# A decoder layer on Trainium2: a pool of its own for the output tile, another order at the start of the last stage, and other PSUM banks for the last blocks

## The chip, the cores and the metric

One core of a Trainium2 chip runs the whole program. The metric is the device time of one execution in microseconds (us); the kernel before took 1507.32 us, the median of three runs (1504.97 to 1509.54). Work is spread over TensorE (PE; its weight loads PEld), VectorE (DVE), ScalarE (ACT), GpSimd (POOL) and SyncE (SP), which only starts DMAs here. A line such as L1580 is line 1580 of the kernel before; the changed kernel counts its lines anew, so that L1277 of before is L1287 of after.

## The reference

One layer of a hybrid decoder in float32, for a prompt of 4096 tokens and a sample batch of 8 x 8 tokens, width 1024:

```python
h = _rmsnorm(x, g_pre)
z = h @ w_in
cb, cc, ch, cg, q, k, v, ag, mq, mg = _split_cols(z)
...
out_b = jax.nn.silu(ag) * o_b      # banded attention, window 128, 8 heads, 2 key-value heads, a sink each
out_c = jax.nn.silu(mg) * o_c      # cross attention into 256 memory tokens, 4 heads
y = jnp.concatenate([out_a, out_b, out_c], axis=-1) @ w_out
return x + _rmsnorm(y, g_post)
```

out_a is a gated short convolution. Keys, values and the last convolution rows are outputs too.

## The kernel before, in words

**Numbers.** Each float32 operand of a large product is split into a rounded part hi and the rest lo, and a product is three matmuls (hi with hi, lo with hi, hi with lo). A tile named mh or hi is the rounded part, ml or lo the rest.

**Stages one to three: the input projection.** The projection is cut into 2 x 2 blocks and done with seven products instead of eight (A for the weights, B for the activations, S and T for sums of them). The tokens go through in eight blocks, the weight columns in three groups. Products gather in PSUM banks as tiles c; DVE and ACT evict them into tiles z (L380, L382), which DMAs store to a tensor qd in DRAM. The first two blocks of tokens are done by a plain scheme (`plain_block`, a table of work by block and step). For block 2 the RMS factor of each row is to stand along the free axis: POOL forms the factors r (L293), `rows_diag` multiplies five columns of them into an identity matrix (L305; the tile is the memory of mix_s, 104 x 104 each), and PE multiplies ones with that (`rows_product`, L314, tile rows_y). In step (1, 4) of the table `rows_diag` stands behind the lo parts of a block of activations (L593) and some sums of weights (L606 to L618).

**The last stage: attention and output projection.** It has 33 blocks of 128 tokens (the 31st to run, b = 30, is followed by the sample block b = 32, then b = 31). A turn of the loop runs `Block.run` of block i: two accumulators y{b}_0 and y{b}_1 of 512 columns, each eight steps k of three matmuls with the weights wo. Between the steps the loop puts other work, by a table of events keyed (p, k): half of the output and step. At (0, 0), `values_and_scores(i)` does the scores of group i+3 (tiles ws in banks 0 to 3, xs in banks 4 and 5) and the values of group i+1 (tile pv, a pair of banks of its own). From group 3 on the softmax weights s are transposed by DVE in 32 x 32 squares and brought into place by 16 DMAs each (w<-s, L1268, on SP); POOL multiplies the cross weights by their reciprocal sums (L1232) and masks w and its copy wd (L1277, `masks`) before PE uses them (`values`). Group 2 is transposed by PE instead (`transposes`, tiles wt in banks 0 and 1, xt in banks 2 and 4, copied out into a tile w by L1286 and L1299).

A block's end: DVE multiplies y by gpost into yn (L1587), ACT sums the squares of y (L1588), and only after that is y's bank free; POOL forms the scale yst (L1601) and adds the scaled yn to the residual xr (L1608); SP stores it. From block 1 on y{b}_1 is the second bank of the pv pair. The tile yn comes from the pool yp, which is opened on memory that earlier tiles leave.

**What sets the order.** DMAs wait in SP's, ACT's or POOL's queue, each in order. A scheduler orders each engine's instructions by their readiness, but those that are issued through `InOrder`, or given to `tc.keep_in_program_order`, stay as written. Before, V (DVE) and TE (PE) were in order from block 1 to block 30 of the loop, S (ACT) only at single calls. In block 0, thus, readiness decided.

**The sample tokens** are worked into blocks 26 to 30 as generators (`sample_mem` twice, `sample_window`), one stage at each event of the table `sample`. They use bank 1 (svnt), 2 (smo) and 3 (sms, smt, smot), and loads svm and place<-in_cmv (L1419) on POOL's queue.

**Loads.** For chunk c (256 tokens) kst and q are loaded by POOL's queue from qd (L1087, L1093) in `chunk_load`, an event of every second block; vh (L1121) by SP.

## Time and profile before

| | us |
|---|---|
| median of three runs | 1507.32 |
| the profiled execution | 1511.43 |
| its span | 1509.7 |
| PE busy | 1475.2 (98%) |
| DVE busy | 1204.0 (80%) |
| ACT busy | 762.1 (50%) |
| POOL busy | 415.5 (28%) |

The mean granted clock of PE is 0.993 of full speed. Instructions are shown with start and length in us, engine, line, operation, output and inputs, shapes and count; behind it in brackets the idle time before it and whose work ended that. Matmuls overlap, so that a row's length can reach over the start of the next.

### The profile page before, as it was taken

Reading aid. Unit: us, or ns where it says so; the run is one execution under the profiler, and the core shown is the slowest. Engines: PE = TensorE matmul, PEld = TensorE weight load, DVE = VectorE, ACT = ScalarE, POOL = GpSimd, SP = SyncE. Lnnn points to the kernel's source line nnn. Section 1 sums busy time; section 2 is a strip of 40 time slices with the busy share of each in tenths; the row PEclk is TensorE's granted clock in tenths of the full one; section 3 lists DMA queues with packets and bytes.
Section 4 is the critical chain, followed back from the end, with each engine's and each line's share of the span. In section 5 each row is a group of like instructions: output and inputs, shape, how many; then the busy total and the mean of one; then the engine's idle time right before and its main releaser. Section 6 shows DMA issues by size and latency. Waiting matters only on the chain.

```text
span 1509.7 us, 30823 instructions
## 1 busy us (share of the span) xinstructions
PE 1475.2 (98%) x11479; PEld 1347.0 (89%) x11479; DVE 1204.0 (80%) x1888; ACT 762.1 (50%) x1878; POOL 415.5 (28%) x557
## 2 busy tenths in 40 slices
PE   9999999999999999999999999899999999999988
PEld 9999999999999999999999999777777777877656
DVE  5769888898998877798677668788888888898733
ACT  5776666466422222244544436556556566556531
POOL 0223322211400000000000111255665565665521
PEclk9999999999999999999999999899999999999999
DMA  9979999887764333388976797978999998998742
GB/s 258 172 244 226 288 277 271 236 284 246 190 221 168 134 121 129 109 276 266 307 226 206 228 281 257 303 203 207 241 238 236 226 223 218 247 229 206 237 127 94
DMA packets 212363, 334.18 MB, mean 221 GB/s; under 512 B 54517, under 2 KB 126197, under 8 KB 212181
## 3 DMA queue, kind: packets, MB, share of 16 engines
q1 hardware_dynamic: 170117, 259.30, 57.2%
q0 software_dynamic: 41376, 71.86, 19.9%
q8 instruction: 91, 1.49, 0.4%
q10 hardware_dynamic: 720, 1.05, 0.2%
q14 instruction: 59, 0.48, 0.1%
HBM read 192.54 MB, written 110.15 MB: 200 GB/s over the span
## 4 chain that ended last, share of the span: by engine, by line
PE 81%; DVE 6%; issue 5%; DMA 4%; ACT 2%; POOL 1%; SPq 0%; DVEq 0%; POOLq 0%; ACTq 0%
PE c L373 50%; PE y L65 19%; PE pv L65 5%; PE ws L65 3%; PE xs L65 1%; DMA wr_0A<-in_w_in 1%; DMA qd<-z 1%; PE mem_acc L789 1%; PE y L1580 1%; DMA vd<-v 1%; DVE s L65 1%; DVE z L380 0%; DVE wo L196 0%; DMA place<-in_xt 0%; ACT s L1207 0%
## 5 line engine op out<-in xcount | busy, mean ns | idle before, releaser
L65 PE MATMUL y<-wo,mh 128*128 128x512 f32 x960 | 307.8, 395 | 0.0
L380 DVE TENSOR_TENSOR z<-c,z 128x520 f32<-128x520 f32 (+1 forms) x308 | 194.3, 644 | 92.9 <-PE c L373 92.1
L65 PEld LDWEIGHTS y<-wo,mh 128*128 128x128 f32 x960 | 180.5, 188 | 51.0 <-issue 4.4
L65 PE MATMUL y<-wo,ml 128*128 128x512 f32 x480 | 187.3, 390 | 0.0
L1207 ACT ACTIVATE s<-s,wnm 128x128 f32<-128x128 f32 x256 | 99.0, 388 | 42.1 <-DVE wnm L65 39.0
L1232 POOL TENSOR_SCALAR s<-s,xrd 128x256 f32<-128x256 f32 x128 | 61.2, 491 | 166.5 <-DVE xrd L65 99.9
L65 PEld LDWEIGHTS y<-wo,ml 128*128 128x128 f32 x480 | 90.3, 188 | 17.6
L1190 ACT COPY s<-ws 128x256 f32<-128x256 f32 x128 | 41.2, 378 | 95.2 <-PE ws L65 74.2
L1608 POOL TENSOR_TENSOR xr<-yn,xr 128x1024 f32<-128x1024 f32 x31 | 74.3, 2397 | 20.8 <-ACT yn L1607 20.6
L748 POOL MEMSET negs<- 128x1 f32 x1 | 0.1, 98 | 264.3 <-PE c L373 264.3
L65 DVE STREAM_TRANSPOSE s<-s 128x1024 f32<-128x1024 f32 x56 | 68.4, 1238 | 2.5 <-POOL s L1232 2.5
L1277 POOL TENSOR_SCALAR_AFFINE_SELECT wd<-w 128x512 f32<-128x512 f32 (+1 forms) x58 | 54.2, 935 | 39.4 <-DMA w<-s 15.2
L1588 ACT ACTIVATE y<-y 128x512 f32<-128x512 f32 (+1 forms) x66 | 38.6, 585 | 52.1 <-DVE yn L65 43.3
L1224 ACT ACTIVATE s<-xs,xnm 128x256 f32<-128x256 f32 x128 | 58.1, 460 | 7.9 <-DVE xnm L1222 7.0
L65 DVE TENSOR_TENSOR yn<-y,gpost 128x512 f32<-128x512 f32 x60 | 41.0, 684 | 24.9 <-PE y L65 23.2
L65 PEld LDWEIGHTS ws<-kst,q 64*128 64x128 f32 x672 | 43.1, 190 | 17.4 <-issue 9.5
L65 PE MATMUL ws<-kst,q 64*128 64x256 f32 x672 | 49.5, 293 | 7.0 <-ACT w L1286 6.5
L65 DVE COPY_PREDICATED s<-wmask,ws 128x256 f32<-128x256 uint8 x112 | 43.5, 441 | 11.8 <-ACT s L1190 7.5
L382 ACT COPY z<-c 128x520 f32<-128x520 f32 (+1 forms) x44 | 24.4, 554 | 54.1 <-PE c L373 51.4
L1607 ACT ACTIVATE yn<-yn,yst 128x1024 f32<-128x1024 f32 x31 | 35.6, 1149 | 27.8 <-POOL yst L1601 27.8
L286 ACT ACTIVATE nat<-nat 104x1024 f32<-104x1024 f32 x40 | 42.2, 1054 | 12.9 <-DMA nat<-in_x_p 12.9
L1207 ACT ACTIVATION_READ_ACCUMULATOR s<-s,wnm 128x1 f32 x256 | 47.9, 187 | 0.0
(995 smaller groups left out, 5015.5 us busy)
## 6 DMA issues: line engine op xcount, KB each, us to landing
w<-s SPq DMA_DIRECT2D x464, 64.0 KB
q<-qd POOLq DMA_DIRECT2D x32, 768.0 KB, 8.2
xr<-in_x_p SPq DMA_DIRECT2D x32, 512.0 KB
nat<-in_x_p SPq DMA_DIRECT2D x39, 416.0 KB
o_yp<-xr SPq DMA_DIRECT2D x31, 512.0 KB
md<-th POOLq DMA_DIRECT2D x48, 260.0 KB, 6.6
qd<-zh SPq DMA_DIRECT2D x48, 260.0 KB
qd<-z SPq DMA_DIRECT2D x48, 260.0 KB
```

Of the source, the lines that this page charges most:

```text
L65: return (lambda *args, **kw: tc.keep_in_program_order(fn(*args, **kw))) if InOrder.on else fn
L286: S.activation(t[:RG], t[:RG], AF.Square, accum_out=r[:RG, i : i + 1])
L373: TE.matmul(bank[:, :HW], l, r, start=first and i == 0, stop=last and i == 3 * KH - 1)
L380: add = lambda dst, other: V.tensor_tensor(dst, c, other, op=ALU.add)
L1190: S.copy(to, squares(s3[:, :, P : 2 * P]))
L1207: S.activation(sm[:, h], sm[:, h], AF.Exp, bias=nm[:, h : h + 1], scale=SCALE, accum_out=den[:, h : h + 1])
L1224: S.activation(p[:, i], s[:, i].rearrange("p (a k j) -> p a k j", a=2, k=4), AF.Exp, bias=nm[:, i : i + 1], scale=SCALE, accum_out=den[:, ...
L1232: G.tensor_scalar(p[:, i], p[:, i], rd[:, i : i + 1], 0.5, op0=ALU.mult, op1=ALU.mult)
L1277: G.affine_select(out, src, pattern=[[32 * sign, 2], [0, 8], [sign, 32]], compare_op=op, fill=0.0, base=base * sign, channel_multiplier=-s ...
L1588: square = lambda acc=acc, p=p, c0=c0, c1=c1, end=end: S.activation((psum(2, "sq") if end else acc)[:m, : c1 - c0], acc[:m], AF.Square, sc ...
L1607: tc.keep_in_program_order(S.mul(yn, yn, st[:, 3:4]))
L1608: G.tensor_tensor(self.xr, yn, self.xr, op=ALU.add)
```

## The change

It has six parts.

1. In step (1, 4) of the plain scheme `rows_diag` goes ahead of the lo parts.
2. The tile yn comes from a new pool yq, opened before the others of its side; the pools vp and yp move with it.
3. Block 0 runs in program order on DVE and PE (`InOrder.on`), and on ACT as well (`InOrder.first`, block 0 alone). Its events are written anew: the transposes of group 2 come first, in banks 2 to 5 (the second cross transpose at (0, 3)), the values and scores at (0, 4); `weights(3)` is taken out of `values_and_scores` and put at (1, 0); the second square transposes of group 3 move to block 1; the split of block 1 is done in two halves.
4. The loads kst and q of chunks from 4 on stay in program order on POOL.
5. In the sample work the svm and cmv loads go to ACT's queue, the copy of smask comes behind the cwv load, svnt uses bank 5, and two stages of the first generator come later: (27, 1, 6) and (28, 0, 5) become (28, 0, 2) and (28, 1, 2). The mix of chunk 15 is loaded at (28, 0, 3) instead of (28, 0, 1).
6. y28_1, y29_1 and y30_1 use bank 5, and the sample block's accumulators banks 3 and 5.

```diff
-            return (lambda *args, **kw: tc.keep_in_program_order(fn(*args, **kw))) if InOrder.on else fn
-    V, TE = InOrder(nc.vector), InOrder(nc.tensor)
+            on = InOrder.first if self.engine is nc.scalar else InOrder.on
+            return (lambda *args, **kw: tc.keep_in_program_order(fn(*args, **kw))) if on else fn
+    V, TE, S = InOrder(nc.vector), InOrder(nc.tensor), InOrder(nc.scalar)
...
-            (1, 4): lambda: [*row, *parts(1, "B22"), *gains(2, "B11"), *sums(2, 1), lambda: rows_diag(), lambda: rows_bank(2),
+            (1, 4): lambda: [*row, lambda: rows_diag(), *parts(1, "B22"), *gains(2, "B11"), *sums(2, 1), lambda: rows_bank(2),
                              *fills(2, "S2"), *row],
...
+        yq = ctx.enter_context(tc.tile_pool(name="yq", bufs=1, side="right"))
         vp = ctx.enter_context(tc.tile_pool(name="vp", bufs=4, side="right"))
         yp = ctx.enter_context(tc.tile_pool(name="yp", bufs=2, side="right"))
...
+        def in_turn(self, ins):
+            if self.c > 3:
+                tc.keep_in_program_order(ins)
...
-                G.dma_start(self.q[:, :, part, :], qd[part, 1:7, :, self.ts].rearrange("j p n -> p j n"))
+                self.in_turn(G.dma_start(self.q[:, :, part, :], qd[part, 1:7, :, self.ts].rearrange("j p n -> p j n")))
...
-        def transposes(self):
+        def transposes(self, n):
+            if n:
+                self.cross_transposes(1, psum(5, f"xt{self.b}_1"))
+                return
...
-                self.band_transposes(u, psum(u, f"wt{self.b}_{u}"))
-            for u in range(2):
-                self.cross_transposes(u, psum(2 + 2 * u, f"xt{self.b}_{u}"))
+                self.band_transposes(u, psum(2 + u, f"wt{self.b}_{u}"))
+            self.cross_transposes(0, psum(4, f"xt{self.b}_0"))
...
-            (S.copy if u else V.tensor_copy)(self.xpt[u], t)
+            (S.copy if u or self.b == 2 else V.tensor_copy)(self.xpt[u], t)
...
-            groups[g].band_weights()
-            for u in range(2):
-                groups[g].cross_weights(u)
+            if i:
+                weights(g)
+            else:
+                blocks[1].split(1)
...
-            G.dma_start(vm[:, j], a["cmv"][j][:, bs])
+            tc.keep_in_program_order(S.dma_start(vm[:, j], a["cmv"][j][:, bs]))
...
-        G.tensor_copy(msk, raw)
...
+        tc.keep_in_program_order(G.tensor_copy(msk, raw))
         svn = vp.tile([P, P], F32, tag="v", name="svn")[:64]
-        transpose_to(svn, [(zs[:, 5, :], 64)], 1, "svnt")
+        transpose_to(svn, [(zs[:, 5, :], 64)], 5, "svnt")
...
-            yn = yp.tile([P, D], F32, tag="yn", name=f"yn{b}", bufs=1)
+            yn = yq.tile([P, D], F32, tag="yn", name=f"yn{b}")
...
+                elif b == 32:
+                    acc = psum(3 + 2 * p, f"y{b}_{p}")
+                elif p == 1 and 28 <= b < 31:
+                    acc = psum(5, f"y{b}_1")
...
-        at(0, 0 if i else 3, values_and_scores, i)
+        if i == 0:
+            at(0, 0, lambda: groups[2].transposes(0))
+            at(0, 3, lambda: groups[2].transposes(1))
+            at(1, 0, weights, 3)
+        if i == 1:
+            at(0, 0, turn, 1, 3)
+        at(0, 0 if i else 4, values_and_scores, i)
...
-        InOrder.on = 0 < i < 31
+        InOrder.on, InOrder.first = i < 31, i == 0
```

**DVE, the plain scheme.** At about 84 us DVE stands at the end of the sums of weights (wa). Before, it goes on like this, where mix_s are the products of `rows_diag` and lo0_1B22 the lo parts:

```order
L614 TENSOR_TENSOR wa2A21_1179<-wa2A11_1185,wa2A21_1179 128x512
L593 TENSOR_SCALAR lo0_1B22_1207<-x0_1B22_813,gpre_61,hi0_1B22_1206 128x260 x4
L606 TENSOR_TENSOR wa2A12_1232<-w0_2A12_451 128x512
L618 TENSOR_TENSOR wa2A12_1232<-wa2A12_1232,wa2A22_1181 128x512
L305 TENSOR_SCALAR mix_s_75<-ident_63,r2_915 104x104 x5
L196 TENSOR_TENSOR w0_2S2_1266<-wa2A22_1181,w0_2S2_1266 128x512
```

In the changed kernel the same place reads:

```order
L615 TENSOR_TENSOR wa2A21_1179<-wa2A11_1185,wa2A21_1179 128x512
L306 TENSOR_SCALAR mix_s_75<-ident_63,r2_915 104x104 x5
L594 TENSOR_SCALAR lo0_1B22_1224<-x0_1B22_813,gpre_61,hi0_1B22_1223 128x260 x4
L607 TENSOR_TENSOR wa2A12_1250<-w0_2A12_451 128x512
L619 TENSOR_TENSOR wa2A12_1250<-wa2A12_1250,wa2A22_1181 128x512
L197 TENSOR_TENSOR w0_2S2_1266<-wa2A22_1181,w0_2S2_1266 128x512
```

mix_s has moved ahead of the four lo parts and two sums of weights.

**PE, the start of the last stage.** Before, PE went from the last product c2_7_2_6 straight to y0_0, and the transposes of group 2 (wt2, xt2) stood inside the second half of block 0:

```order
L1580 MATMUL y0_1_12254<-wo1_1_11952,ml0_11992 128x512
L1580 MATMUL y0_1_12254<-wo1_1_11952,mh0_11991 128x512
L1285 MATMUL wt2_0_12263<-ident_63,s2_11356 128x128 x4
L1285 MATMUL wt2_1_12272<-ident_63,s2_11356 128x128 x4
L1298 MATMUL xt2_0_12280<-ident_63,s2_11356 128x128 x4
L1298 MATMUL xt2_1_12286<-ident_63,s2_11356 128x128 x4
L1580 MATMUL y0_1_12254<-wo2_1_11955,mh0_11991 128x512
```

In the changed kernel they follow the last product, where L66 is the line of the wrapper that keeps the order:

```order
L374 MATMUL c2_7_2_6_12020<-hi2_7T4_11919,w2_2A22_8593 128x260
L66 MATMUL wt2_0_12132<-ident_63,s2_11356 128x128 x4
L66 MATMUL wt2_1_12141<-ident_63,s2_11356 128x128 x4
L66 MATMUL xt2_0_12149<-ident_63,s2_11356 128x128 x4
L66 MATMUL y0_0_12129<-wo0_0_11764,mh0_11991 128x512
L66 MATMUL y0_0_12129<-wo0_0_11764,ml0_11992 128x512
```

Three of the four transposes have moved ahead of all of y0_0; xt2_1 comes behind its third step.

**POOL, a pair of blocks in the middle.** Before, the loads of chunk 5 (kst5, q5) stand around the addition to xr3, ahead of the weights of s7 (xrd are reciprocal sums); AFFINE_SELECT are the masks:

```order
L1601 TENSOR_TENSOR yst3_12749<-yst3_12749,mhalf_70 128x1
L1087 DMA kst5_13083<-qd_150 128x2x384
L1093 DMA q5_13085<-qd_150 128x6x256
L1608 TENSOR_TENSOR xr3_12452<-yn3_12748,xr3_12452 128x1024
L1093 DMA q5_13085<-qd_150 128x6x256
L1232 TENSOR_SCALAR s7_12959<-s7_12959,xrd7_0_13055 128x2x4x32 x2
L1232 TENSOR_SCALAR s7_12959<-s7_12959,xrd7_1_13063 128x2x4x32 x2
L1277 AFFINE_SELECT wd6_13117<-w6_12916 128x512
```

In the changed kernel:

```order
L1624 TENSOR_TENSOR yst3_12752<-yst3_12752,mhalf_70 128x1
L1631 TENSOR_TENSOR xr3_12455<-yn3_12751,xr3_12455 128x1024
L1240 TENSOR_SCALAR s7_12962<-s7_12962,xrd7_0_13058 128x2x4x32 x2
L1240 TENSOR_SCALAR s7_12962<-s7_12962,xrd7_1_13066 128x2x4x32 x2
L1089 DMA kst5_13086<-qd_150 128x2x384
L1099 DMA q5_13088<-qd_150 128x6x256 x2
L1287 AFFINE_SELECT wd6_13120<-w6_12919 128x512
```

The three loads have moved behind the weights of s7 and stand right ahead of the masks of group 6.

More of the change, by code (lines that the diff above doesn't have):

```diff
@@ L53, in hybrid_layer @@
     nc = tc.nc
-    S, G, DMA = nc.scalar, nc.gpsimd, nc.sync
+    G, DMA = nc.gpsimd, nc.sync
     class InOrder:
-        on = False
+        on = first = False
         def __init__(self, engine):
@@ L1012, in open_attention @@
     def open_attention():
-        nonlocal ps, mixp, wp, wl, vp, bp, bq, yp
+        nonlocal ps, mixp, wp, wl, vp, bp, bq, yp, yq
         own.close()
@@ L1165, in scores @@
             self.crosses(cross)
+            if self.b == 3:
+                blocks[1].split(0)
             self.band_softmax()
@@ L1368, in values_and_scores, with weights @@
                 groups[g].cross_softmax(cross[u], u)
-            groups[g].band_weights()
-            for u in range(2):
-                groups[g].cross_weights(u)
+            if i:
+                weights(g)
+            else:
+                blocks[1].split(1)
+    def weights(g):
+        groups[g].band_weights()
+        for u in range(2):
+            groups[g].cross_weights(u)
     tails = []
@@ L1555, in split @@
             src = chunks[b // 2].mix[:, :, (b % 2) * P : (b % 2) * P + P]
-            hi, lo = parts(f"mh{b}"), parts(f"ml{b}")
-            copy = S.copy(hi, src)
-            if 0 < b < 31:
-                tc.keep_in_program_order(copy)
-            V.tensor_tensor(lo, src, f(hi), op=ALU.subtract)
-            self.hl = [hi, lo]
+            if part != 1:
+                self.hl = hi, lo = parts(f"mh{b}"), parts(f"ml{b}")
+                copy = S.copy(hi, src)
+                if 1 < b < 31:
+                    tc.keep_in_program_order(copy)
+            if part != 0:
+                hi, lo = self.hl
+                V.tensor_tensor(lo, src, f(hi), op=ALU.subtract)
         def run(self, last, events):
             b, m = self.b, self.m
-            yn = yp.tile([P, D], F32, tag="yn", name=f"yn{b}", bufs=1)
+            yn = yq.tile([P, D], F32, tag="yn", name=f"yn{b}")
             dst = a["o_ys"] if b == 32 else a["o_yp"][b * P : (b + 1) * P, :]
@@ L1649, in events_of @@
             if i == 28:
-                at(0, 1, lambda: chunks[15].load_mix())
+                at(0, 3, lambda: chunks[15].load_mix())
         elif (i + 3) // 2 < NCH - 1:
             at(0, 3, lambda: chunks[(i + 3) // 2].load_mix())
-        if i == 0:
-            at(1, 2, lambda: groups[2].transposes())
         at(1, 1, turn, 2, i + 2)
@@ L1658, in events_of @@
         at(1, 2, turn, 0, i + 3)
-        at(1, 2, turn, 1, i + 3)
-        if i + 1 < len(blocks) and blocks[i + 1].b != 32:
-            at(1, 3 if i else 4, blocks[i + 1].split)
+        if i:
+            at(1, 2, turn, 1, i + 3)
+            if i + 1 < len(blocks) and blocks[i + 1].b != 32:
+                at(1, 3, blocks[i + 1].split)
         for (n, p, k), stage in sample.items():
```

8 lines of the change are left out of this document (4 added, 4 removed).

## The prediction

> **What bounds the kernel now.** I read the list of waits of TensorE first, then a table of stretches of the span, then the timelines around the three stretches that stand out. A row of waits gives who waited on which line, for whom, and total us, times, longest.
>
> ```profile
> PE pv L65 <- ACT y L1588: 6.7, 4, 4.2
> PE ws L65 <- ACT w L1286: 6.5, 1, 6.5
> PE rows_y L314 <- DVE mix_s L305: 2.2, 1, 2.2
> PE pv L65 <- POOL w L1277: 1.8, 2, 1.2
> PE y L1580 <- ACT y L1588: 1.6, 1, 1.6
> PE sws L65 <- ACT svn L1398: 1.4, 1, 1.4
> ```
>
> These six groups are 20.2 us. The page's first part has PE busy 1475.2 of 1509.7 us, so all its idle time is 34.5 us, and nothing can be won but that and what a lowered clock costs behind it. In the table, the columns behind a stretch are its length, the busy us of PE, PEld, DVE, ACT and POOL, the granted clock, the DMA share and GB/s.
>
> ```profile
> 86.00:94.00 8.00, 6.00 (x34) 5.83 (x35) 4.87 (x12) 5.38 (x11) 0.00 (x0) 0.79 0.87 236
> 970.00:982.00 12.00, 5.38 (x40) 4.66 (x42) 9.19 (x19) 8.24 (x29) 6.27 (x11) 0.62 1.28 363
> 1006.00:1400.00 394.00, 393.01 (x2844) 310.52 (x2844) 348.22 (x613) 235.56 (x856) 232.15 (x294) 1.00 0.91 227
> 1440.00:1452.00 12.00, 7.77 (x43) 5.04 (x42) 4.99 (x7) 3.32 (x6) 4.11 (x4) 0.72 0.59 153
> 1464.00:1500.00 36.00, 32.88 (x178) 25.70 (x177) 12.89 (x28) 9.25 (x18) 6.43 (x5) 1.00 0.26 88
> ```
>
> From 1006 to 1400 us PE idles 1.0 us of 394: the middle of the last stage is bound by TensorE's own work, which the change leaves as it is, so a gain must come from elsewhere. Three short stretches ran at a granted clock of 0.79, 0.62 and 0.72, each behind a PE gap of over 2 us. I call them A (86 us), B (970 us) and C (the end, from 1400 us); the change touches all three, and the middle as well.
>
> **A: the five mix_s products ahead of the lo parts.**
>
> ```profile
> 81.15 1.51 POOL L293 TENSOR_TENSOR r<-r,mhalf 104x5 f32<-104x5 f32 x1
> 84.29 1.68 DVE L593 SCALAR_TENSOR_TENSOR lo_1B<-x_1B,gpre,hi_1B 128x260 fp32r<-128x260 f32 x4
> 87.22 1.00 DVE L305 TENSOR_SCALAR mix_s<-ident,r 104x104 f32<-104x104 f32 x5
> 88.00 1.38 PE L314 MATMUL rows_y<-mix_s,ones 104*128 104x260 f32 x4 [2.25 <-DVE mix_s L305]
> ```
>
> The factors are there at 82.66 (81.15 + 1.51), and DVE reaches this place at 84.3. With mix_s first it runs from 84.3 to 85.3; PE wants it at 88.00 - 2.25 = 85.75. The gap of 2.25 us goes, and with it the clock drop, 8.00 x (1 - 0.79) = 1.7 us: 3.9 us in all. The four lo parts come 1.0 us later; their readers on PE stand behind rows_y and the w_1A and w_2A products with the part before, and these hide it; without that cover it costs 1.0 us. No instruction is added. I take **3.5 us**, between 2.9 and 3.9.
>
> **B: the start of the last stage.**
>
> ```profile
> 953.85 0.28 PE L373 MATMUL c<-hi_7T,w_2A 128*128 128x260 f32 x1
> 956.53 0.42 DVE L380 TENSOR_TENSOR z<-c,z 128x260 f32<-128x260 f32 x1
> 969.28 0.39 PE L1580 MATMUL y<-wo,mh 128*128 128x512 f32 x1
> 970.85 0.69 DVE L1587 TENSOR_TENSOR yn<-y,gpost 128x512 f32<-128x512 f32 x1 [6.48 <-DMA qd<-z]
> 975.57 1.05 ACT L1286 COPY w<-wt 128x512 f32<-128x512 f32 x2
> 976.19 2.13 PE L65 MATMUL ws<-kst,q 64*128 64x256 f32 x13 [6.53 <-ACT w L1286]
> 985.01 0.50 PE L65 MATMUL y<-wo,mh 128*128 128x512 f32 x1
> ```
>
> The chain reads backwards: ws4 waits 6.53 us for bank 0, which the copy of wt2 frees; ACT comes to that copy only at 975.57, since its exponentials waited for DVE; and DVE sat 6.48 us at yn0, whose memory lay over z tiles still being stored. With a pool of its own yn0 waits no longer. The copy of wt2 comes ahead of the scores on ACT, and the transposes use banks 2 to 5, so ws4 needs no release from them.
>
> What is late next is at the front. The first transposes now stand ahead of y0_0, in a bank that the last projection tile leaves by DVE's z eviction, done at 956.95, whereas PE ends its products at 954.13. Before, y0_0 filled these 2.8 us; now PE idles there. Its work from there to the old gap is the same and took 969.67 - 954.13 = 15.5 us, so PE is through at 957.0 + 15.5 = 972.5.
>
> The next group, ws4 to y1, took 985.01 - 976.19 = 8.8 us at a lowered clock and with a 0.43 us wait. What it takes at full clock is shown one block on:
>
> ```profile
> 996.11 1.70 PE L65 MATMUL ws<-kst,q 64*128 64x256 f32 x24
> 998.46 1.09 PE L65 MATMUL pv<-w,mv 128*64 128x128 f32 x16
> 999.38 1.03 PE L65 MATMUL pv<-w,vh 128*64 128x256 f32 x8
> 1000.94 0.50 PE L65 MATMUL y<-wo,mh 128*128 128x512 f32 x1
> 994.49 2.26 POOL L1277 TENSOR_SCALAR_AFFINE_SELECT w<-w 128x512 f32<-128x512 f32 x2
> ```
>
> It is 1000.94 - 996.11 = 4.8 us. y1 would start at 972.5 + 4.8 = 977.3. One wait is left in between: bank 3 holds y0_1 until DVE's product (0.69) and ACT's Square (0.58, row at 1443.85 below) have followed its last matmul, about 1.3 us: 978.6, or 985.0 - 978.6 = 6.4 us earlier. Two things may eat of this. The masks of w3 ended at 996.75 with their reader at 999.38, a cover of 2.6 us; a reader that comes 6.4 us sooner waits up to 3.8 us, unless the loads ahead of the masks come sooner too. They follow DVE work that stood behind yn0's wait, so they move by most of it: I take 0.7. And a gap of 2.8 us can lower the clock, as 2.25 us did at A for 1.7 us, while the two gaps of 1.6 us between 1464 and 1500 (clock 1.00) did not: two in five, 0.7 us. B gives **5.0 us**; its ends are 1 (3.8 and 1.7 lost) and 8 (most of the new gap gone).
>
> The Trainium skill ("TensorE: Matmul & The Clock Gate", section "Part 1: The HAM clock gate (the "warmup" mystery)") puts the drop behind at least one idle window of about 3.4 us. By it A's gap of 2.25 us would not have lowered the clock, and the row with 0.79 says that it did; for the new gap at 954 the rule gives no drop and B 5.7, by the row at A up to 1.7 us more is lost and B is 4.0. I go by the row.
>
> **The middle: POOL's loads.** For the twelve chunks from 4 on, three load issues move on POOL to between the weights of s and the masks. A row of a line gives min/median/max ns.
>
> ```profile
> L1093 POOL DMA_DIRECT2D q<-qd x32: 818/858/928, 718.4 to 1357.2; - x32
> 1137.56 1.84 POOL L1232 TENSOR_SCALAR s<-s,xrd 128x256 f32<-128x256 f32 x4 [4.64 <-DVE xrd L65]
> 1140.56 2.61 POOL L1277 TENSOR_SCALAR_AFFINE_SELECT wd<-w 128x512 f32<-128x512 f32 x2 [1.16 <-DMA o_yp<-xr]
> 1143.23 1.39 POOL L1277 TENSOR_SCALAR_AFFINE_SELECT w<-w 128x512 f32<-128x512 f32 x2
> 1144.17 1.17 PE L65 MATMUL pv<-w,vh 128*64 128x256 f32 x8
> ```
>
> The issues of a chunk (kst once, q twice) take about 3 x 0.86 = 2.6 us. Weights end at 1139.40, so masks could start at 1142.0, not 1140.56. The first w mask ended at 1143.93 and PE read at 1144.17: the cover is 0.24 us. Full shift: 1.44 - 0.24 = 1.2 us a block, 14 us for twelve. But the wd pair took 2.61 us here and 1.51 us at 992.91 to 994.42 in another block, so in part it was waiting in any case; 1.5 us from 1142.0 ends at 1143.5, 0.3 us later than before, about 0.1 over the cover. That is the nearer row. On the other side the loads no longer share the DMA engines with the w loads that precede these masks, which may end an idle us there. I take **-1.5 us**, ends -14 and +1. The loads themselves are read two blocks later or more, and come late for nobody.
>
> **C: the end.**
>
> ```profile
> 1439.69 2.36 DVE L65 STREAM_TRANSPOSE s<-s 128x1024 f32<-128x1024 f32 x2
> 1441.97 1.18 DVE L65 TENSOR_TENSOR ml<-place,mh 128x1024 fp32r<-128x1024 f32 x1
> 1443.08 0.68 DVE L65 TENSOR_TENSOR yn<-y,gpost 128x512 f32<-128x512 f32 x1
> 1443.85 0.58 ACT L1588 ACTIVATE y<-y 128x512 f32<-128x512 f32 x1 [2.36 <-DVE yn L65]
> 1444.59 1.98 PE L65 MATMUL pv<-w,mv 128*64 128x128 f32 x16 [4.23 <-ACT y L1588]
> 1449.26 0.79 PE L65 MATMUL y<-wo,mh 128*128 128x512 f32 x1
> 1457.40 1.40 POOL L1277 TENSOR_SCALAR_AFFINE_SELECT w<-w 128x512 f32<-128x512 f32 x2
> 1466.28 1.09 PE L65 MATMUL pv<-w,mv 128*64 128x128 f32 x16 [1.56 <-ACT y L1588]
> ```
>
> y28_1 lies in the pair of banks that pv30 needs, and its Square waits for DVE behind transposes and a subtraction. With y28_1 to y30_1 in bank 5, pv30 and pv31 wait for nothing of them: 4.23 + 1.56 us. pv30 took 1449.26 - 1444.59 = 4.7 us at the lowered clock against 1000.94 - 998.46 = 2.5 us above: 2.2 us more. y32 in banks 3 and 5 takes the 1.55 us wait of L1580; svnt in bank 5 the 1.36 us of sws; and the svm loads on ACT's queue with the smask copy behind its use free POOL for the masks, 1.8 us. Sum: 4.23 + 1.56 + 2.2 + 1.55 + 1.36 + 1.8 = 12.7 us.
>
> Late next: without its waits PE reaches pv31 at 1440.36 + 2.5 + (1464.7 - 1449.3) = 1458.3, and its second group reads w about 0.9 us later, at 1459.2; w's last mask ended at 1458.80. That cover of 0.4 us goes if PE gains the 3.2 us ahead of 1440 (1.36 + 1.8) and the s31 chain doesn't: a wait of 0 to 2.8 us. ACT now holds two load issues ahead of the Square of y28_1 (0.86 us each on POOL above), about 1.7 us; who waits for that Square is y29_1 in bank 5, some 5 us later. I take off 1.5 us for pv31 and 1.7 us for such waits of the sample rows (smo0, smot0 and y32, one step later each; each is one gap of the kind at 1466): **C = 9.5 us**, ends 4 and 12.7.
>
> **Sum.** 3.5 + 5.0 - 1.5 + 9.5 = 16.5 us. The profiled run took 1511.43 us for a span of 1509.7; it would be 1494.9. It stands 4.1 us above the median of 1507.32, so a median of 1490.8, say **1491 us** (-1.1%).
>
> **The rivals.**
> *The next wait takes the place of the old ones.* B keeps 1 us because masks and clock eat the rest, C 4 because w31's masks and DVE's list end the waits instead, A 3.5, the middle -2: 6.5 us, 1501 us. For it: DVE is the engine behind most of these waits and its work isn't less. Against it: the covers worked out above.
> *Slower: the masks fall behind the loads.* In each of twelve blocks the masks start the full 2.6 us later, because the w loads that they wait for move as well: (2.6 - 0.24) x 12 = 28 us, against 18 us from A, B and C: 1517 us. It decides from 18 / 12 + 0.24 = 1.7 us a block. For it: a cover of 0.24 us. Against: the masks already waited 1.16 us behind s for a DMA, under which nearly half of the issues lie.
> *The waits don't move.* yn0's release or the banks at the end turn out to hang on something else that ends at the same time, and A's gain is eaten by DMA in the next phase: within 4 us of before, 1506 us.
>
> **Chances.** Forecast 0.68, next wait 0.17, masks 0.07, no movement 0.08. A measurement of this kernel can tell about 0.3% (4.5 us) from no change, so faster 0.85, same 0.08, slower 0.07. The forecast's own ends are 1482 (3.9 + 8 + 12.7 + 1 = 25.6 us) and 1500. To leave out no more than 2 in 10 the range takes in the second rival: 1482 to 1503.
>
> **What would show it.** A: no gap ahead of rows_y, and a clock of 1.00 around 86. B: DVE's wait at yn0 gone, a gap of 2 to 3 us ahead of wt2, and y1 about 6 us earlier, measured from the last c. C: pv30 and pv31 with no wait for y. The middle: masks at most 0.4 us later against pv. Wrong would be many new waits of pv for w's masks between 1000 and 1400, or a wait of wt2 for far more than the eviction.

## The result, and the profile after

The changed kernel takes 1520.25 us, the median of 5 runs (1517.47 to 1523.84), against 1507.32 us for the kernel before in 5 runs beside it (1504.52 to 1511.5). The ratio is 1.0085, with a 95% interval of 1.0059 to 1.0111. So it is slower by 0.85%; a faster kernel, at 1491 us, was predicted. Its profiled execution took 1523.84 us, with a span of 1522.1, 12.4 us longer than that of before.

First, the list of waits of TensorE in the changed kernel: who waited, for whom, and in us the total, the number of waits and the longest.

```profile
PE pv L66 <- ACT y L1611: 14.4, 6, 5.1
PE y L66 <- ACT svn L1415: 9.5, 1, 9.5
PE pv L66 <- DMA o_yp<-xr: 3.4, 1, 3.4
PE wt L66 <- DVE z L381: 2.8, 1, 2.8
```

The waits of before for w (6.5 us), for rows_y (2.2) and for the masks (1.8) no longer lead the list. But pv waits for a Square of y six times instead of four, and for 14.4 us instead of 6.7; and a wait that did not exist, for the copy of svn, is the longest of all. The third row is of the same kind as the first: that pv starts at 1284.66, right behind a Square whose last row ends at 1284.61. The stretches of the changed kernel show where these lie, in the columns of the prediction's table (length, busy us of PE, PEld, DVE, ACT and POOL, granted clock, DMA share, GB/s):

```profile
86.00:94.00 8.00, 7.95 (x63) 7.66 (x62) 7.16 (x12) 5.30 (x11) 0.23 (x1) 1.00 0.88 229
993.00:1398.00 405.00, 391.23 (x2784) 307.64 (x2780) 330.01 (x599) 230.29 (x839) 216.77 (x277) 0.98 0.84 217
1112.00:1126.00 14.00, 13.40 (x68) 10.02 (x69) 9.71 (x23) 8.90 (x33) 8.13 (x12) 0.77 0.63 166
1445.00:1460.00 15.00, 5.55 (x16) 4.07 (x15) 8.47 (x19) 4.69 (x15) 2.83 (x4) 0.66 0.81 275
```

The second row runs from the values of group 3 to those of group 27, 25 blocks; the same blocks of the kernel before are this stretch:

```profile
998.00:1384.00 386.00, 385.01 (x2790) 303.85 (x2787) 341.16 (x601) 230.80 (x841) 226.78 (x275) 1.00 0.92 227
```

What took 386 us takes 405. PE idled 1.0 us there and now idles 13.8, and the same work keeps it busy for 391.2 instead of 385.0 us, at a clock of 0.98 (0.77 in the stretch of 1112 to 1126, behind one of the new gaps): 12.8 + 6.2 = 19 us. At 86 us, in contrast, the gap and the drop of the clock are gone. And at 1445 PE works 5.55 of 15 us, in a stretch that was to be free of waits.

The next table cuts each profiled execution at the start of the values (pv, the 16 matmuls from w and mv) of some groups, and at the last product c of the projection. It gives the us between one mark and the next:

| kernel | to last c | to values 2 | to values 3 | to 27 | to 29 | to 30 | to 31 | to last matmul |
|---|---|---|---|---|---|---|---|---|
| before | 954.1 | 27.5 | 16.8 | 386.0 | 35.7 | 24.4 | 21.7 | 37.5 |
| after | 949.7 | 21.6 | 21.4 | 405.5 | 34.0 | 30.9 | 17.2 | 35.6 |
| e3_both | 954.2 | 21.7 | 22.6 | 388.4 | 33.7 | 18.6 | 20.2 | 35.6 |
| e4_before_in_turn | 955.2 | 29.4 | 17.2 | 401.2 | 34.7 | 25.9 | 20.4 | 37.5 |
| e8_end_alone | 948.7 | 25.8 | 16.2 | 387.9 | 33.6 | 18.7 | 19.9 | 35.7 |
| e10_loads_odd | 956.2 | 23.3 | 18.8 | 384.0 | 33.7 | 18.7 | 21.7 | 35.6 |
| e11_mix2_later | 949.0 | 23.3 | 16.5 | 389.7 | 33.7 | 18.7 | 21.8 | 35.7 |

By it the changed kernel gains 4.4 us ahead of the last stage, 5.9 up to the values of group 2, gives 4.6 back at those of group 3, loses 19.5 in the middle, and gains 1.7 - 6.5 + 4.5 + 1.9 = 1.6 at the end: a loss of 12.2 us. The first column tells nothing of the change: it is 948.7 in e8, which lacks part 1, and 956.2 in e10, which has it.

**One turn of the middle.** These are rows of POOL, SP, ACT and PE of the changed kernel in the turn that holds one of the new gaps. The DMAs w<-s bring the transposed weights from the tile s into w; the COPY of ACT then fills the same s with the next scores.

```profile
1092.54 12.21 SPq L1278 DMA_DIRECT2D w<-s  x16
1099.70 1.85 POOL L1240 TENSOR_SCALAR s<-s,xrd 128x256 f32<-128x256 f32 x4 [2.77 <-DVE xrd L66]
1101.50 0.80 POOL L1089 DMA_DIRECT2D kst<-qd  x1
1102.31 1.66 POOL L1099 DMA_DIRECT2D q<-qd  x2
1104.85 0.52 SPq L1632 DMA_DIRECT2D o_yp<-xr  x1
1111.29 1.52 POOL L1287 TENSOR_SCALAR_AFFINE_SELECT wd<-w 128x512 f32<-128x512 f32 x2 [7.32 <-DMA w<-s]
1111.30 0.65 ACT L1198 COPY s<-ws 128x256 f32<-128x256 f32 x2 [9.06 <-DMA w<-s]
1111.83 0.60 ACT L1611 ACTIVATE y<-y 128x512 f32<-128x512 f32 x1
1112.60 1.98 PE L66 MATMUL pv<-w,mv 128*64 128x128 f32 x16 [5.11 <-ACT y L1611]
1112.77 0.34 SPq L1560 DMA_DIRECT2D xr<-in_x_p  x1
```

POOL has issued the three loads (1.9 MB) by 1103.97. The 16 w loads of the group at hand are issued from 1092.54 to 1104.75, and the trace also records when each has landed. The six that were issued from 1098.15 to 1101.24 landed 1.9 to 2.1 us later; the last four, issued from 1101.87 on, beside POOL's loads, took 4.4 to 7.2 us, and the last landed at 1111.00. Behind that the masks of POOL and the copy of ACT start, after 7.32 and 9.06 us of waiting. The Square of y stands behind this copy on ACT, and pv behind the Square, for the bank that y holds. pv reads w itself as well, so of its 5.11 us some 3.5 are the w loads directly and 1.6 the way over ACT. SP is held too, from 1107.13 to 1112.77, ahead of its load of xr, by the store o_yp.

In the kernel before the loads ran beside the w loads of such a turn too, but they were issued from 1095.82, behind the fifth of the 16: the last w load landed at 1109.42, and pv at 1111.01 did not wait. Part 4 thus changed when the two meet. Nor do they meet like this in each of the twelve blocks: PE has five gaps of over 1 us in the middle of the changed kernel, at 1091, 1113, 1230, 1265 and 1285, of 13.6 us together.

**The end.** Rows of PE and ACT of the changed kernel around the wait of 9.45 us:

```profile
1440.69 0.30 PE L66 MATMUL svnt<-ident,zs 128*64 128x128 f32 x1
1450.31 0.44 ACT L1522 ACTIVATE ssm<-ssm,swnm 128x192 f32<-128x192 f32 x1
1452.98 0.58 ACT L1611 ACTIVATE y<-y 128x512 f32<-128x512 f32 x1 [2.14 <-DVE yn L66]
1453.57 1.04 ACT L1575 CAST mh<-place 128x1024 fp32r<-128x1024 f32 x1
1454.51 0.26 ACT L1415 COPY svn<-svnt 64x128 f32<-64x128 f32 x1
1454.82 0.80 PE L66 MATMUL y<-wo,mh 128*128 128x512 f32 x1 [9.45 <-ACT svn L1415]
```

PE writes svnt into bank 5 at 1440.69. ACT copies it out only at 1454.51, behind the softmax of the sample window, the Square of y28_0 and the split of a block. y28_1, which now uses bank 5 too, waits for that copy, and stands ahead of everything else on PE.

### The profile page after: what moved, and what is told of

Same layout as the page of the kernel before. It is cut to its first block, busy times and chain, and to the rows that moved or that the text cites. A ratio compares the mean times of both kernels' runs of the same rounds, so it can differ in the third digit from the quotient of the medians.

```text
span 1522.1 us, 30808 instructions
## 1 busy us (share of the span) xinstructions
PE 1476.1 (97%) x11479; PEld 1346.2 (88%) x11479; DVE 1191.7 (78%) x1887; ACT 762.1 (50%) x1879; POOL 400.8 (26%) x553
## 4 chain that ended last, share of the span: by engine, by line
PE 61%; DMA 18%; SPq 6%; DVE 6%; issue 4%; ACT 3%; POOL 1%; ACTq 0%; DVEq 0%; POOLq 0%
PE c L374 44%; PE y L66 10%; DMA xr<-in_x_p 6%; SPq L1278 6%; DMA o_yp<-xr 3%; PE pv L66 2%; DMA nat<-in_x_p 2%; DMA place<-in_xt 2%; DMA w<-s 1%; PE y L1603 1%; PE ws L66 1%; DMA place<-md 1%; DMA wr_3A<-in_w_in 1%; DVE s L66 1%; PE mem_acc L790 1%
## 5 line engine op out<-in xcount | busy, mean ns | idle before, releaser
L66 PE MATMUL y<-wo,mh 128*128 128x512 f32 x992 | 321.0, 398 | 9.5 <-ACT svn L1415 9.5
L66 PEld LDWEIGHTS y<-wo,mh 128*128 128x128 f32 x992 | 187.9, 189 | 63.5 <-ACT svn L1415 9.9
L66 PE MATMUL y<-wo,ml 128*128 128x512 f32 x496 | 194.5, 392 | 0.0
L66 PEld LDWEIGHTS y<-wo,ml 128*128 128x128 f32 x496 | 94.2, 190 | 18.2
L1215 ACT ACTIVATE s<-s,wnm 128x128 f32<-128x128 f32 x248 | 95.9, 388 | 26.8 <-DVE wnm L66 23.7
L66 DVE COPY_PREDICATED s<-wmask,ws 128x256 f32<-128x256 uint8 x116 | 45.0, 441 | 34.6 <-ACT s L1198 30.0
L66 DVE STREAM_TRANSPOSE s<-s 128x1024 f32<-128x1024 f32 x58 | 70.2, 1231 | 2.4 <-POOL s L1240 2.4
L66 DVE TENSOR_TENSOR yn<-y,gpost 128x512 f32<-128x512 f32 x62 | 42.4, 684 | 36.6 <-PE y L66 34.4
L1287 POOL TENSOR_SCALAR_AFFINE_SELECT wd<-w 128x512 f32<-128x512 f32 (+1 forms) x58 | 44.6, 770 | 74.9 <-DMA w<-s 57.4
L66 PEld LDWEIGHTS ws<-kst,q 64*128 64x128 f32 x696 | 43.4, 186 | 11.0 <-issue 10.2
L66 PE MATMUL pv<-w,mv 128*64 128x128 f32 x480 | 34.6, 289 | 17.8 <-ACT y L1611 14.4
L1630 ACT ACTIVATE yn<-yn,yst 128x1024 f32<-128x1024 f32 x31 | 35.6, 1150 | 32.1 <-POOL yst L1624 32.1
L383 ACT COPY z<-c 128x520 f32<-128x520 f32 (+1 forms) x44 | 24.4, 554 | 53.5 <-PE c L374 50.8
L66 PE MATMUL ws<-kst,q 64*128 64x256 f32 x696 | 49.7, 288 | 0.5 <-DMA q<-qd 0.5
```

The source lines that it names most:

```text
L66: return (lambda *args, **kw: tc.keep_in_program_order(fn(*args, **kw))) if on else fn
L1215: S.activation(sm[:, h], sm[:, h], AF.Exp, bias=nm[:, h : h + 1], scale=SCALE, accum_out=den[:, h : h + 1])
L1287: G.affine_select(out, src, pattern=[[32 * sign, 2], [0, 8], [sign, 32]], compare_op=op, fill=0.0, base=base * sign, channel_multiplier=-s ...
```

## The experiments

The theory after this reading: part 4 (kst and q in program order) costs the middle, because the *transfers* of these loads now run beside the last w loads of a turn, and bank 5 costs the end, because svnt and y28_1 meet there. The first rival for the middle is the prediction's own, that POOL's *issues* hold back the masks. A second is that another part of the change (block 0's order, the pool yq) made the middle slow. Ratios below are to the kernel before on the same chip, with 95% intervals. Its median was 1506.39 us beside the first four kernels, 1509.18 beside the next four and 1507.34 beside the last three. A percentage turned into us uses 1507.

### Part 4 and bank 5, each undone

**e1_loads_free** is the changed kernel without part 4, so that the scheduler places kst and q again:

```diff
         def in_turn(self, ins):
-            if self.c > 3:
-                tc.keep_in_program_order(ins)
+            return
```

> The changed kernel without part 4: the loads kst and q are left to the scheduler, which puts them back ahead of the weights of s. Theory one (the moved loads cost the middle: the six gaps of pv behind the Square of y between 989 and 1285 us, 17.2 us, and the lowered clock behind them): about 1520 - 20 = 1500 us, and none of these gaps. Rival (the middle suffers from the order on SyncE, where vh and xr loads moved, or from the start of the stage): 1520 us, the gaps stay.

Measured: 1506.54 us, ratio 0.9988 (0.997 to 1.0005). Its middle (values 3 to 27) takes 387.5 us.

**e2_svnt_bank1** is the changed kernel with svnt back in bank 1:

```diff
-        transpose_to(svn, [(zs[:, 5, :], 64)], 5, "svnt")
+        transpose_to(svn, [(zs[:, 5, :], 64)], 1, "svnt")
```

> The changed kernel with svnt in bank 1 as before. Theory (y28_1 waited 9.45 us in bank 5 for svn's copy, which stands on ScalarE behind the softmax of the sample window): the gap goes, with 2.5 us of lowered clock, and 1.4 us come back at sws: 1520 - 9.45 - 2.5 + 1.4 = 1509.5 us. Rival (another wait at the same place is just as long, the list of VectorE): 1517 us or more.

Measured: 1515.13 us, ratio 1.0049 (1.0025 to 1.0072). The stretch between the values of 29 and 30 takes 18.7 us instead of 30.9; the middle stays at 405.7.

**e3_both** has both edits.

> Both edits together: loads left to the scheduler and svnt in bank 1. If the two losses are all that the prediction missed: 1520 - 20 - 10.5 = 1489 us, near the forecast of 1491. If one of the theories is wrong: 1500 to 1510 us.

Measured: 1496.79 us, ratio 0.9943 (0.9921 to 0.9965). The middle takes 388.4 us and the stretch to the values of 30 18.6. The stretch at the end of e3, for comparison with the last row of the changed kernel's:

```profile
1438.00:1462.00 24.00, 21.34 (x161) 14.72 (x159) 11.95 (x26) 8.77 (x21) 6.28 (x7) 1.00 0.70 214
```

What follows: without these two faults the kernel is faster by 0.57%. All three came out slower than expected (1500, 1509.5 and 1489 us), by 5.6 to 8 us, so the two faults are not all that was missed. Undoing part 4 is worth 0.0097 and 0.0106 (after to e1, e2 to e3), 15 to 16 us; moving svnt back 0.0036 and 0.0045, 5.4 to 6.8 us; by the intervals of the single ratios each of these is uncertain by some 4 to 5 us. The wait of y28_1 was 9.45 us and lowered the clock (0.66 over 1445 to 1460); of the 12.2 us by which e2 shortens that stretch, 4.2 come back at the values of 31, which take 21.4 us instead of 17.2, as they did before the change (21.7).

**e4_before_in_turn** is the other direction: the kernel before, with part 4 and nothing else.

```diff
-            G.dma_start(self.kst[:, :, lo:], qd[:, 0, ...])
+            self.in_turn(G.dma_start(self.kst[:, :, lo:], qd[:, 0, ...]))
...
-                G.dma_start(self.q[:, :, part, :], qd[part, 1:7, ...])
+                self.in_turn(G.dma_start(self.q[:, :, part, :], qd[part, 1:7, ...]))
```

> The kernel before with part 4 alone: kst and q of chunks from 4 on stay behind the weights of s. Theory one: the middle loses 15 to 20 us, 1523 to 1527 us, with pv waiting for the Square of y. Rival: 1507 us, no such gaps.

Measured: 1529.17 us, ratio 1.0132 (1.0097 to 1.0168): 20 us for the order of three issues in twelve blocks. The middle of e4, then its waits of PE and ACT:

```profile
1001.00:1402.00 401.00, 388.44 (x2786) 306.25 (x2784) 330.27 (x600) 230.10 (x841) 213.57 (x276) 0.99 0.84 218
```

```profile
PE pv L65 <- ACT y L1592: 13.0, 5, 4.6
PE pv L65 <- DMA o_yp<-xr: 4.3, 1, 4.3
...
ACT s L1194 <- DMA w<-s: 28.2, 4, 8.6
```

These are the waits of the changed kernel, without its other five parts, so the second rival falls. The copies of ACT for the next scores waited for w loads 28.2 us in e4; the same row of the changed kernel and of the kernel before:

```profile
ACT s L1198 <- DMA w<-s: 37.8, 6, 9.1
```

```profile
ACT s L1190 <- DMA w<-s: 6.9, 2, 4.4
```

The three kernels with part 4 as it stands have 28 to 45 us in this row (e2: 45.4); of the others only e12, below, has over 14.2.

### The issue or the transfer

**e5_tiny_loads** is the kernel before, its loads unmoved, with three further loads of 2 KB each in the place where part 4 puts kst and q, kept in program order, in the same twelve blocks:

```diff
+            if c > 3:
+                for n in range(3):
+                    tc.keep_in_program_order(G.dma_start(tiny.tile([P, 4], F32, tag="few", name=f"few{c}_{n}"), a["x_p"][0:P, 0:4]))
```

> The kernel before, with three loads of 2 KB each issued by GpSimd in twelve blocks at the very place to which part 4 moves kst and q (behind the weights of s, ahead of the masks); kst and q stay where they were. It separates the issues from the transfers. Theory one-a (the transfers of kst and q, 1.9 MB, delay the w loads that the next turn needs): the issues cost at most some 0.1 us a block, 1507 to 1509 us, no gaps of pv behind the Square of y in the middle. Rival, as the prediction had it (the masks fall behind the issues): about 1520 us or more, with masks late by 2 us.

Measured: 1510.28 us, ratio 0.9999 (0.9982 to 1.0016). One of its turns, on POOL:

```profile
1106.93 1.84 POOL L1232 TENSOR_SCALAR s<-s,xrd 128x256 f32<-128x256 f32 x4 [4.66 <-DVE xrd L65]
1108.73 1.70 POOL L1388 DMA_DIRECT2D few<-in_x_p  x3
1111.08 1.52 POOL L1277 TENSOR_SCALAR_AFFINE_SELECT wd<-w 128x512 f32<-128x512 f32 x2 [0.65 <-DMA w<-s]
```

What follows: the three issues take 1.70 us of POOL and the masks wait 0.65 us for w loads even behind them. The rival of the issues falls: the issues stand in what was waiting time, as the prediction had it, and cost nothing that this interval (2.7 us either way) can show. The transfers, and when they run, are left of part 4. (Its real issues take 2.5 us, 0.8 more than these; that much was not tried by itself.)

**e10_loads_odd** is e2 with the loads kept in program order at the same point of a turn, but in the odd turns, one block later:

```diff
+        if i == 0:
+            at(0, 4, chunk_load, 3)
+        if i % 2 and i > 1:
+            at(0, 1, chunk_load, (i + 5) // 2)
...
-            at(0, 1 if i else 4, chunk_load, i // 2 + 3)
```

> The changed kernel with svnt in bank 1 and part 4 kept (loads in program order, behind the weights of s and ahead of the masks), but one block later, in the odd blocks. Theory one-a (what counts is which w loads, residual loads and stores the 1.9 MB of kst and q run beside on the DMA engines, and how much slack those have): here they run beside the 16 w loads of the even groups' turn from their start, as in the kernel before, so the middle costs no more than 388 us from the values of group 3 to those of group 27, against 405 in the run with svnt in bank 1: about 1498 us. Rival (a place right behind the weights and ahead of the masks is bad in any block): 1515 us, as that run.

Measured: 1495.97 us, ratio 0.9923 (0.99 to 0.9945), the lowest of all kernels here, though the intervals of e3, e8 and e11 overlap with it. Its middle, and two stretches of 12 us in it: an even turn, where the loads of the changed kernel would be, and the odd turn with the loads:

```profile
998.00:1382.00 384.00, 383.78 (x2782) 305.55 (x2784) 333.67 (x601) 230.57 (x842) 216.19 (x277) 1.00 0.92 227
1099.00:1111.00 12.00, 12.00 (x80) 10.02 (x78) 9.71 (x17) 6.92 (x29) 6.33 (x9) 1.00 0.90 191
1122.00:1134.00 12.00, 12.00 (x100) 9.43 (x99) 11.09 (x22) 8.22 (x31) 9.11 (x11) 1.00 1.35 323
```

PE has no gap left in the middle (0.2 us of 384). The DMA share is the mean busy time of the core's 16 DMA engines by their packets, as a share of the stretch; it can exceed 1, as packets overlap. In the odd turn it is 1.35 and nothing waits. In the turn of the changed kernel shown above it was 1.20:

```profile
1101.00:1113.00 12.00, 6.89 (x59) 5.71 (x59) 4.78 (x8) 2.94 (x9) 4.53 (x8) 0.94 1.20 261
```

So it is not the load on the DMA engines as such, but what is due beside it. The rows of e10 tell these turns apart:

```profile
1092.36 13.54 SPq L1278 DMA_DIRECT2D w<-s  x16
1107.69 1.51 POOL L1287 TENSOR_SCALAR_AFFINE_SELECT wd<-w 128x512 f32<-128x512 f32 x2 [2.43 <-DMA w<-s]
...
1122.85 0.80 POOL L1089 DMA_DIRECT2D kst<-qd  x1
1124.25 12.51 SPq L1278 DMA_DIRECT2D w<-s  x16
1139.40 1.52 POOL L1287 TENSOR_SCALAR_AFFINE_SELECT wd<-w 128x512 f32<-128x512 f32 x2 [2.25 <-DMA w<-s]
```

In the even turn the w loads are issued up to 1105.90; the last four land 2.0 to 2.2 us after their issue, the last at 1107.31, and the masks start upon it at 1107.69. No time is left there, and it was beside these last loads that the changed kernel put 1.9 MB in the turn shown above. In the odd turn the loads go at 1122.85, when the w loads for the next masks have landed (the last at 1120.19), and ahead of another 16. The first eight of these land only 7.0 to 7.5 us after their issue, but the last four after 2.9 to 4.2, and all by 1139.11: the masks start at 1139.40, and pv at 1143.07 does not wait. The Trainium skill ("DMA: Bandwidth & Descriptors", section "Queues, rings and completion order") says that each DMA engine takes turns between the queues that have work for it, a packet at a time; that fits w loads on SP's queue that come late beside loads on POOL's, while no run here separates the packets of the two. The median time of a q load from issue to landing grew from 8.2 us to 11.0 in the changed kernel and is 11.1 in e10, so that a slow q is not what costs.

In the turn shown of the changed kernel, then, the w loads are the first to be late, and the store o_yp, issued behind them, follows. Other turns lose their time one step earlier. SP's own list of waits says how long the issue of w loads stood until an xr load had landed; in order the kernel before, the changed kernel, e4 and e10:

```profile
SPq L1268 <- DMA xr<-in_x_p: 7.5, 12, 1.8
SPq L1278 <- DMA xr<-in_x_p: 36.2, 19, 4.0
SPq L1272 <- DMA xr<-in_x_p: 24.7, 16, 2.9
SPq L1278 <- DMA xr<-in_x_p: 3.2, 3, 2.1
```

In the middle of the kernel before kst is issued some 4 us behind the xr load (0.5 MB) of its turn, and that xr load lands 4.5 to 7.0 us after its issue. In nine of the twelve blocks of the changed kernel kst comes 1.4 to 5.7 us ahead of the xr load, which then takes 7.5 to 9.4 us; in e10 the two mostly go within 1 us of each other, and xr takes 4.4 to 5.9. At the gaps of 1091 and 1230 this was the delay: SP stood for about 3 us until xr had landed, at 1083.90 and at 1221.62, and issued the rest of the 16 w loads only then. No run moved the xr load by itself, so that its share of the 20 us is open.

### The other parts alone

**e6_diag_alone** is the kernel before with part 1:

```diff
-            (1, 4): lambda: [*row, *parts(1, "B22"), *gains(2, "B11"), *sums(2, 1), lambda: rows_diag(), lambda: rows_bank(2),
+            (1, 4): lambda: [*row, lambda: rows_diag(), *parts(1, "B22"), *gains(2, "B11"), *sums(2, 1), lambda: rows_bank(2),
```

> The kernel before with part 1 alone. Theory: the gap of 2.25 us ahead of rows_y and 1.7 us of lowered clock go, 1507 - 3.5 = 1503.5 us. Rival, from the trace of both edits: the wait moves to the product behind rows_y, which waits for its eviction on ScalarE (rb), as long as before: 1507 us.

Measured: 1506.75 us, ratio 0.9983 (0.9963 to 1.0003): a gain of 2.6 us whose interval just reaches no change.

**e7_start_alone** is the kernel before with parts 2 and 3: the pool yq and the order of block 0. Its core:

```diff
+        yq = ctx.enter_context(tc.tile_pool(name="yq", bufs=1, side="right"))
...
-            yn = yp.tile([P, D], F32, tag="yn", name=f"yn{b}", bufs=1)
+            yn = yq.tile([P, D], F32, tag="yn", name=f"yn{b}")
...
+        if i == 0:
+            at(0, 0, lambda: groups[2].transposes(0))
+            at(0, 3, lambda: groups[2].transposes(1))
+            at(1, 0, weights, 3)
```

> The kernel before with parts 2 and 3 alone. Theory: the values of group 2 come 5 to 6 us earlier after the last product of the projection, but 3.5 to 6 us of it are given back two groups on, where pv waits for the Square of y1 behind copies of scores that wait for the w loads of group 3: 1505 to 1506 us. Rival: the give-back came from part 4 or the end, and the start alone brings the forecast 5 us: 1502 us.

Measured: 1510.43 us, ratio 1.0001 (0.9982 to 1.002). The values of group 2 come 21.7 us behind the last c instead of 27.5, those of group 3 21.6 us behind them instead of 16.8, and the middle takes 389.8 instead of 386.0.

**e8_end_alone** is the kernel before with parts 5 and 6, but with svnt left in bank 1:

```diff
-            G.dma_start(vm[:, j], a["cmv"][j][:, bs])
+            tc.keep_in_program_order(S.dma_start(vm[:, j], a["cmv"][j][:, bs]))
...
+                elif b == 32:
+                    acc = psum(3 + 2 * p, f"y{b}_{p}")
+                elif p == 1 and 28 <= b < 31:
+                    acc = psum(5, f"y{b}_1")
```

> The kernel before with parts 5 and 6 alone, but svnt left in bank 1. Theory: the end gains what the prediction gave it, 9 to 11 us: 1496 to 1498 us. Rival: the end's gain in the run with both edits hangs on the earlier parts: 1502 us.

Measured: 1500.15 us, ratio 0.9948 (0.9924 to 0.9971): a gain of 7.8 us (4.4 to 11.5), the largest of any part.

What follows: the pieces add up. Part 1 -2.6, parts 2 and 3 +0.2, part 4 +19.9, the end -7.8 and svnt in bank 5 about +6 make +15.7 us, against +12.9 measured for all of them. Each piece is uncertain by some 3 to 5 us.

### The start, once more

Why do the 5.9 us of the start not stay? These rows of SP, ACT and PE are from e3, whose middle is free of part 4:

```profile
973.51 0.38 SPq L1106 DMA_DIRECT2D place<-md  x1
973.93 5.83 SPq L1126 DMA_DIRECT2D vh<-vn  x1
979.88 15.68 SPq L1277 DMA_DIRECT2D w<-s  x16
997.25 0.65 ACT L1197 COPY s<-ws 128x256 f32<-128x256 f32 x2 [8.45 <-DMA w<-s]
998.55 1.98 PE L66 MATMUL pv<-w,mv 128*64 128x128 f32 x16 [4.78 <-ACT y L1610]
```

And the same 16 loads of w for group 3 in the kernel before:

```profile
979.14 10.47 SPq L1268 DMA_DIRECT2D w<-s  x16
```

The w loads start no earlier than before, because SP stands 5.83 us at the issue of one small load behind the mix load of 1 MB (place<-md), and they take 15.68 us to issue instead of 10.47. For 5.7 of these SP waited, at the seventh w load, until that mix load had landed. The copy of ACT waits for the w loads, the Square behind it, and pv 4.78 us for that.

**e11_mix2_later** is e3 with that mix load of chunk 2 kept behind the w loads:

```diff
-            DMA.dma_start(self.mix, md[:, :, self.ts].rearrange("k p n -> p k n"))
+            ins = DMA.dma_start(self.mix, md[:, :, self.ts].rearrange("k p n -> p k n"))
+            if self.c == 2:
+                tc.keep_in_program_order(ins)
```

> Both edits together (loads left to the scheduler, svnt in bank 1), and the load of chunk 2's mix, 1 MB, kept in program order on SyncE, so that the 16 w loads of group 3 go ahead of it. Theory (at the start of the stage, what was won is given back because these w loads stand behind the mix load): the gap of 4.8 us ahead of the values of group 3 shrinks to under 1 us, with the lowered clock behind it, and the run comes to 1497 - 5 = 1492 us. Rival (the loads q and kst of chunks 2 to 4 slow the w loads whatever the order): the gap stays above 3 us, 1497 us.

Measured: 1496.66 us, ratio 0.9932 (0.9913 to 0.995), which its interval cannot tell from e3. The values of group 3 come 16.5 us behind those of group 2 instead of 22.6, so the mix load was what held them. But values 2 come 1.6 us later, the middle takes 1.3 us longer and the stretch to the values of 31 1.6 more, and the total shows nothing of the gain. Each of these is one profile; whether the wait only moved, or the rest differs from execution to execution, was not shown.

**e12_all** has the edits of e10 and e11 together.

> The changed kernel with svnt in bank 1, the loads kst and q in program order in the odd blocks, and the mix load of chunk 2 behind the w loads of group 3. If both theories of the two runs beside it hold: 1490 to 1493 us, near the forecast. If only one: 1497 us.

Measured: 1501.63 us, ratio 0.9966 (0.9945 to 0.9988), slower than either by 0.3 to 0.4%, with intervals that touch. The two edits do not add up. In its trace the order of e10 is lost: in eight blocks kst is issued 1.6 to 3.2 us ahead of the xr load again, and SP's w loads wait 21.6 us for xr loads, against 3.2 in e10. What that costs the profile does not say: the profiled execution took 1497.66 us, one of the fastest of twelve from 1495.22 to 1511.18 and less than the profiled one of e10 (1499.89), and its middle takes 389.4 us, as in e11 (389.7). Why the two edits together lose the order is open.

## Why the prediction was wrong, point by point

**The middle: the step that failed.** The prediction said that "the loads no longer share the DMA engines with the w loads that precede these masks, which may end an idle us there", and took -1.5 us. Only POOL's time was worked out to a price; the 1.9 MB were counted as leaving a crowded place, and not as arriving at another. Where they arrive, they delay SP's xr load and the w loads behind it, or, in the turn shown, the last four w loads, of which the last landed 3.5 us after PE was ready for it. Nor are the masks, the only reader that the prediction looked at, the last to let PE go: pv reads w itself, and the tile s is written by the next scores, that copy stands on ACT ahead of a Square, and the Square frees pv's bank. The sign that the prediction named, waits of pv for w's masks, thus did not appear. The step cost 19.5 us in the profile, 20 us by e4 and 15 to 16 by e1 and e3. The lower end of -14, worked out from full POOL shifts, was near in size and wrong in kind. So was the rival "the masks fall behind the loads", which gave 1517 us at a chance of 0.07: its time is nearly that measured, by luck, since its price (2.6 us of issues over a cover of 0.24 a block) is refuted by e5. It did name the w loads that the masks wait for, but had them move with the issues and not slowed by the transfers.

**The end: two lines of one list that meet.** The prediction credited "svnt in bank 5 the 1.36 us of sws" and, in the same sum, "y28_1 to y30_1 in bank 5 [...] wait for nothing of them". Both were true of the old waits. That svnt and y28_1 now stand in one bank one behind the other, and that the copy between them is late on ACT, was not asked. Without this (e8, bank 1) the end gave 7.8 us, and 11.1 us in the stages of e3, against 9.5 predicted, ends 4 and 12.7: the rest of that step held. Bank 5 was not even needed for the 1.36 us of sws: with svnt in bank 1 the lists of e2, e3 and e8 show no wait of sws either.

**B: right up to the next turn.** The new gap ahead of wt is 2.81 us (2.8 predicted), and the values of group 2 come 5.9 us earlier, measured from the last c. The prediction allowed 0.7 us for the masks of w3 because "the loads ahead of the masks come sooner too". They did not: SP's queue held them. 4.6 us went at the values of group 3, and e7 measures a total of nothing (a gain of -3.0 to +2.7 us by its interval), where the prediction had 5.0 and a lower end of 1.

**A: right, and smaller.** Predicted 3.5 us (2.9 to 3.9), measured 2.6. The wait for mix_s fell from 2.25 us to at most 0.9 in the profiles of after, e3 and e6. But with part 1 a wait for the next eviction on ACT, of the tile rb, takes its place in some profiles: 2.2 us in e3 and 2.4 in e10. And the gap is not there in every execution of a kernel without part 1: four of the five profiled ones have it, with 2.1 to 2.9 us, and the fifth is e8. This is the place in e8; PE has no gap in it:

```profile
84.00:94.00 10.00, 10.00 (x83) 9.88 (x82) 5.65 (x11) 6.33 (x15) 1.15 (x2) 1.00 0.80 204
```

The prediction took the gap of one profile for that of every execution.

**Sum.** With 2.6 + 0 - 20 + 1.6 for 3.5 + 5.0 - 1.5 + 9.5, 16.5 us of gain become a loss of 16, near the 13 measured. The prediction's own lower ends, 2.9 + 1 - 14 + 4, also add up to a loss, of 6 us or about 1513 us; it gave 1500 as that end, which these numbers do not make. The range ended at 1503 since the mechanism that could pass it was given 7 in 100, on the strength of a cover on one engine.

## What to carry to other kernels

A moved load has two prices: the issue on its queue, and the bytes beside whatever is due when they arrive; look at the tightest DMA of the turn it moves into and at the large loads that it now goes ahead of, and follow that tile not only to its reader but to whoever writes its source next. When several tiles are given the same free bank in one change, line up their lifetimes against each other, not only against the old waits. And a wait taken out ahead of work that waits for transfers can come back in the next turn (here 4.6 us of 5.9), so price it at the end of that turn.

## What the runs showed of the hardware that was not expected

A gap on PE of one length lowers the granted clock in some executions and not in others. The new gap ahead of wt was 2.8 to 2.9 us in all eight profiled kernels that have it. In three of them (e1, e10, e11) the clock fell behind it, in five not. Two stretches of 4 us from behind that gap, of e1 and of the changed kernel:

```profile
954.00:958.00 4.00, 4.00 (x18) 3.52 (x19) 3.50 (x6) 2.09 (x4) 2.03 (x3) 0.63 0.92 332
```

```profile
954.00:958.00 4.00, 4.00 (x31) 3.18 (x31) 2.07 (x4) 2.16 (x4) 3.46 (x5) 1.00 0.73 200
```

PE worked through all of both stretches, at 0.63 of its speed in the first and at full speed in the second. So what a removed gap of 2 to 3 us returns behind it, some 1.7 us by the prediction's row at A, differs from execution to execution, and one profile of before is one draw of it. Three in eight is close to the two in five that the prediction took for this gap.

The issue of a DMA can take long by itself: SP's small load of vh took 5.83 us to issue behind 1 MB of mix in e3, against 0.41 us for another in the middle of the changed kernel, and all that was queued behind it waited without showing a releaser.
